# Rotary embedding on one core: sixteen positions to a partition, and four transfers that move two tiles each

## The chip, the core and the metric

The kernel runs on one core of a Trainium2 chip. The metric is the device time of one execution in microseconds. The engines named below are TensorE (PE, matmuls; its weight loads are PEld), VectorE (DVE), ScalarE (ACT), GpSimd (POOL) and SyncE (SP), which here only issues DMAs. The core has 16 DMA engines that move data between HBM and SBUF. SBUF is the working memory of 128 partitions; PSUM is the smaller memory that TensorE writes; GpSimd's work here is all in SBUF.

## The reference: what is computed

`x` is float32 of shape (16, 512, 1024): 16 batches, 512 positions, 16 heads of 64 values. `cos` and `sin` are (512, 32), one row for each position, the same for every batch and head. Each head's 64 values are two halves, x1 and x2:

```python
x1, x2 = (x[..., :half_dim].copy(), x[..., half_dim:].copy())
rotated = np.concatenate([x1 * cos - x2 * sin, x1 * sin + x2 * cos], axis=-1)
```

So the output is x times cos, plus x with its halves swapped times a signed sine (minus sine for the first half, plus sine for the second). 33.55 MB are read and 33.55 MB written, and every value needs two products and one sum.

## The kernel before

**Tiling.** There are 8 tiles of 4 MB, `x_tiles[0..7]`, each [128 partitions, 8 rows of 1024]. A partition holds 8 consecutive positions of one batch (64 partitions to a batch, two batches to a tile), so a partition's part of a tile is one run of 32 KB in HBM, and a whole tile is one contiguous block there. Five SBUF buffers hold the tiles; tiles 5, 6 and 7 reuse those of tiles 0, 1 and 2. Results are written over x in place and stored from there.

**Tables.** `tabs` holds 64 rows each of cos and sin (8 positions to a row). Two matmuls with the selection matrix `sel` (L115) spread them to all 128 partitions in PSUM. `tab` is one PSUM bank: half of it is the cosine table; behind that lies `snp`, the signed sine of the rows of group 2 alone. `sns` in SBUF is the signed sine of all rows, filled by ACT (L120, L121). PSUM is full: one bank for `tab`, six for `pp`, one for `ps`.

**The work on a tile.** `GROUPS` names stretches of rows (first row, number of rows) and `PLAN[t]` is an order written out by hand for each tile. An entry is a letter and a group:

- T (L148): POOL multiplies the swapped halves by `sns` into a T buffer. B (L148): the same on DVE, with `snp` from PSUM.
- P (L151): DVE multiplies x by the cosine into `pp` in PSUM. S (L153): DVE adds T and pp over x.
- A (L155): DVE multiplies x by the cosine in place. M (L160 to L163): for each chunk of 512 columns TensorE adds T and x into `ps` with two identity matmuls, and ACT copies the sum over x. There is one `ps`, so the chunks go one after the other: matmul of T, matmul of x, copy.

So a group is finished either by T (or B), P and S, or by T, A and M. The T buffers come from two pools of two, one for groups of two rows and one for groups of three: a T waits until the user of the buffer two before it is done. Each engine works its instructions in order.

**DMAs.** All x transfers are issued by SP in order, on one queue: the loads of tiles 0 (in four cuts) to 4, two tiny transfers `few` (L97), stores 0, 1, 2, loads 5, 6, 7, stores 3 to 6, and tile 7 in two cuts. A load into a reused buffer waits for the store that empties it. Every DMA takes the next of eight completion semaphores in turn and waits until the DMA that used it eight before has landed; the tiny transfers use up turns, so that a store does not inherit the semaphore of a transfer that is still far from done.

Of the kernel before, what the change touches and what calls it, by code (L numbers as in the profile page):

```python
# [11 lines left out]
@with_exitstack  # L12
def kernel(
    ctx: ExitStack,
    tc: tile.TileContext,
    x: bass.AP,
    cos: bass.AP,
    sin: bass.AP,
    num_heads: bass.AP,
    out: bass.AP,  # L20
):
    nc = tc.nc
    P = nc.NUM_PARTITIONS
    batch, seq, dim = x.shape
    nh = num_heads
    hd = dim // nh
    half = hd // 2


    BP = 2  # L30
    HP = P // BP
    R = seq // HP
    NT = batch // BP
    NB = 5
    C = 512
    GP = 3
    assert HP * R == seq and BP * NT == batch

    GROUPS = [(0, 3), (3, 3), (6, 2), (0, 2), (2, 2), (4, 2), (3, 2), (5, 3)]
    PLAN = ["T3 P3 T4 S3 P4 S4 B2 T5 P5 S5 P2 S2",
            "T0 T2 T1 P0 S0 P1 A2 M2 S1",
            "T0 T1 P0 B2 S0 P2 S2 P1 S1",
            "T2 T0 T1 A2 M2 P0 S0 P1 S1",
            "T0 T1 P0 B2 S0 A2 M2 P1 S1",
            "T0 T2 T1 P0 S0 A2 M2 P1 S1",
            "T2 T0 T1 A2 M2 P0 S0 P1 S1",
            "T0 T6 T7 P0 S0 P6 S6 P7 S7"]

    xv = x.rearrange("b (p r) d -> (b p) (r d)", r=R)
    xv = xv.rearrange("(t p) f -> t p f", p=P)
    ov = out.rearrange("b (p r) h d -> (b p) (r h d)", r=R)
    ov = ov.rearrange("(t p) f -> t p f", p=P)
    cosv = cos.rearrange("(p r) j -> p (r j)", r=R)
    sinv = sin.rearrange("(p r) j -> p (r j)", r=R)

    fixed = ctx.enter_context(tc.tile_pool(name="fixed", bufs=1))
    xin = ctx.enter_context(tc.tile_pool(name="xin", bufs=1))
    tpools = {n: ctx.enter_context(tc.tile_pool(name=f"tpool{n}", bufs=2)) for n in sorted({n for _, n in GROUPS})}  # L60
    ptab = ctx.enter_context(tc.tile_pool(name="ptab", bufs=1, space=bass.MemoryType.PSUM))
    pgrp = ctx.enter_context(tc.tile_pool(name="pgrp", bufs=1, space=bass.MemoryType.PSUM))
    prow = ctx.enter_context(tc.tile_pool(name="prow", bufs=1, space=bass.MemoryType.PSUM))

    ctx.enter_context(tc.manual_schedule())

    SYNC = mybir.DependencyInfo(mybir.DependencyClass.Sync, mybir.DependencyReason.DATA)

    def implied(inst, *others):
        for o in others:  # L70
            tc.declare_no_dep(inst.ins, o.ins, reason="implied by an earlier wait of the engine")

    bufs = [xin.tile([P, R * dim], FP32, name=f"x{i}_sb") for i in range(NB)]
    x_tiles = [bufs[t % NB] for t in range(NT)]
    loads = [[] for _ in range(NT)]
    stores = [[] for _ in range(NT)]

    def load(t, *cuts):
        for a, b in cuts or ((0, R),):
            loads[t].append(nc.sync.dma_start(out=x_tiles[t][:, a * dim:b * dim], in_=xv[t][:, a * dim:b * dim]))  # L80

    def store(t, *cuts):
        for a, b in cuts or ((0, R),):
            stores[t].append(nc.sync.dma_start(out=ov[t][:, a * dim:b * dim], in_=x_tiles[t][:, a * dim:b * dim]))

    load(0, (0, 1))
    tabs = fixed.tile([HP, 2, R * half], FP32, name="tabs")
    nc.scalar.dma_start(out=tabs[:, 1], in_=sinv)
    nc.scalar.dma_start(out=tabs[:, 0], in_=cosv)
    load(0, (1, 2), (2, 4), (4, 8))  # L90
    for t in range(1, NB):
        load(t)


    few = fixed.tile([1, 2], FP32, name="few")
    for i in range(2):
        nc.sync.dma_start(out=few[:, i:i + 1], in_=cosv[:1, i:i + 1])  # L97

    ident = fixed.tile([P, P], FP32, name="ident")
    nc.gpsimd.memset(ident, 0.0)  # L100
    nc.gpsimd.affine_select(  # L101
        out=ident, in_=ident, compare_op=ALU.not_equal, fill=1.0,
        base=0, pattern=[[-1, P]], channel_multiplier=1,
    )
    i64 = ident[:HP, :HP]
    sel = fixed.tile([HP, P], FP32, name="sel")
    nc.gpsimd.tensor_copy(out=sel.rearrange("k (b p) -> k b p", b=BP),  # L107
                          in_=bass.AP(tensor=i64.tensor, offset=i64.offset, ap=[i64.ap[0], [0, BP], [1, HP]]))

    tab = ptab.tile([P, C], FP32, name="tab")  # L110
    cos_ps = tab[:, :R * half].rearrange("p (r j) -> p r j", r=R)
    PR, PN = GROUPS[2]
    snp = tab[:, R * half:R * half + PN * hd].rearrange("p (r s j) -> p r s j", r=PN, s=2)
    sin_ps = pgrp.tile([P, GP * dim], FP32, name="pp")[:, :R * half].rearrange("p (r j) -> p r j", r=R)
    spread = [nc.tensor.matmul(out=o.rearrange("p r j -> p (r j)"), lhsT=sel, rhs=tabs[:, i],  # L115
                               start=True, stop=True) for i, o in ((1, sin_ps), (0, cos_ps))]
    sns = fixed.tile([P, R, 2, half], FP32, name="sns")
    signed = []
    for o, r0 in ((sns, 0), (snp, PR)):
        signed.append(nc.scalar.copy(out=o[:, :, 1, :], in_=sin_ps[:, r0:r0 + o.shape[1], :]))  # L120
        signed.append(nc.scalar.mul(out=o[:, :, 0, :], in_=sin_ps[:, r0:r0 + o.shape[1], :], mul=-1.0))  # L121

    def view(t, k):
        r0, n = GROUPS[k]
        return x_tiles[t][:, r0 * dim:(r0 + n) * dim]

    def cosb(k):
        r0, n = GROUPS[k]
        return bass.AP(tensor=cos_ps.tensor, offset=cos_ps.offset + r0 * half,
                       ap=[cos_ps.ap[0], [half, n], [0, 2 * nh], [1, half]])  # L130

    def snb(tab, r0, n):
        return bass.AP(tensor=tab.tensor, offset=tab.offset + r0 * hd, ap=[tab.ap[0], [hd, n], [0, nh], [1, hd]])

    def swapped(xr, n):
        return bass.AP(tensor=xr.tensor, offset=xr.offset + half, ap=[xr.ap[0], [hd, n * nh], [-half, 2], [1, half]])

    Ts, pps = {}, {}

    def emit(t, op):  # L140
        o, k = op[0], int(op[1])
        r0, n = GROUPS[k]
        xr = view(t, k)
        if o in "TB":
            m = GP if t == 0 and o == "T" else n
            Ts[t, k] = tpools[m].tile([P, m * dim], FP32, name="T")[:, :n * dim]
            eng, tb = (nc.gpsimd, snb(sns, r0, n)) if o == "T" else (nc.vector, snb(snp, r0 - PR, n))
            return [eng.tensor_tensor(out=Ts[t, k], in0=swapped(xr, n), in1=tb, op=ALU.mult)]  # L148
        if o == "P":
            pps[t, k] = pgrp.tile([P, GP * dim], FP32, name="pp")[:, :n * dim]  # L150
            return [nc.vector.tensor_tensor(out=pps[t, k], in0=xr, in1=cosb(k), op=ALU.mult)]  # L151
        if o == "S":
            return [nc.vector.tensor_tensor(out=xr, in0=Ts[t, k], in1=pps[t, k], op=ALU.add)]  # L153
        if o == "A":
            return [nc.vector.tensor_tensor(out=xr, in0=xr, in1=cosb(k), op=ALU.mult)]  # L155
        made = []
        for c in range(n * dim // C):
            ps = prow.tile([P, C], FP32, name="ps")
            xc = xr[:, c * C:(c + 1) * C]
            made.append(nc.tensor.matmul(out=ps, lhsT=ident, rhs=Ts[t, k][:, c * C:(c + 1) * C],  # L160
                                         start=True, stop=False))
            made.append(nc.tensor.matmul(out=ps, lhsT=ident, rhs=xc, start=False, stop=True))  # L162
            made.append(nc.scalar.copy(out=xc, in_=ps))  # L163
        return made

    done = [[] for _ in range(NT)]

    def compute(t):
        met = False
        for op in PLAN[t].split():  # L170

            met = met or op[0] in "SA"
            for i in emit(t, op):
                if t > 0 and met and op[0] != "T":
                    implied(i, *loads[t])
                if t >= NB:
                    implied(i, *loads[t - NB], *stores[t - NB], *done[t - NB])
                done[t].append(i)

    for t in range(NB):  # L180
        compute(t)
        if t < NT - NB:
            store(t)
    for t in range(NB, NT):
        load(t)
    for t in range(NT - NB, NB):
        store(t)
    for t in range(NB, NT):
        compute(t)
        store(t, *((0, 5), (5, 8)) if t == NT - 1 else ())  # L190


# [33 lines left out]
```

## Time and profile before

| what | value |
|---|---|
| median of 3 runs | 162.48 us (162.45 to 162.59) |
| the profiled execution's own time | 162.54 us |
| its span | 160.8 us |
| DVE busy | 138.4 us (86%) |
| POOL busy | 130.2 us (81%) |
| PE busy | 58.4 us (36%) |
| ACT busy | 14.1 us (9%) |
| moved, mean rate over the span | 67.25 MB, 418 GB/s |
| mean granted TensorE clock | 0.795 |

Busy time is that of instructions; the span runs from the first to the last of them. In the slices the span is cut into 40 equal parts of 4.02 us, and a digit is the busy share in tenths. The lines for groups of instructions give busy time and the mean duration in ns, then the engine's idle time before them and what ended it. A DMA is issued by its queue (SPq) and its bytes follow later, behind everything issued earlier; it has landed when its semaphore is complete.

### The profile page before, as it was taken

The numbers are of one execution on the slowest core, as the hardware profiler recorded it, in microseconds if no ns is written. First come the engines' busy times: TensorE is split into PE (matmuls) and PEld (weight loads), VectorE is DVE, ScalarE is ACT, GpSimd is POOL, SyncE is SP. The second block draws the span as 40 slices with busy tenths as digits, with TensorE's granted clock in tenths as the row PEclk, the third lists the DMA queues.
The fourth block names the chain that finished last, engine by engine and source line by source line (L and its number), as shares of the span: only waits on it lengthen the run. The fifth ranks groups of instructions, "written<-read, shape, count | busy, mean of one in ns | idle before, by whom it ended". The sixth has DMA issues, their size and how long they took to land.

```text
span 160.8 us, 390 instructions
## 1 busy us (share of the span) xinstructions
PE 58.4 (36%) x84; PEld 18.3 (11%) x84; DVE 138.4 (86%) x48; ACT 14.1 (9%) x25; POOL 130.2 (81%) x29
## 2 busy tenths in 40 slices
PE   0500000022388803088701368896868630000000
PEld 0200000010122100022201022222222200000000
DVE  0069999999999999999999999999999999999200
ACT  3110000000011110011200011002121210000000
POOL 2299929999999899995999299999999999991000
PEclk9999999999999995557995555559999995555555
DMA  5999999999999999999999999999999999999994
GB/s 159 383 444 481 391 448 465 391 432 473 400 400 506 400 391 481 432 391 481 432 391 448 465 391 432 473 400 408 497 400 400 483 416 408 473 424 400 428 417 199
DMA packets 3046, 67.25 MB, mean 418 GB/s; under 512 B 357, under 2 KB 485, under 8 KB 741
## 3 DMA queue, kind: packets, MB, share of 16 engines
q1 hardware_dynamic: 2884, 67.11, 97.8%
q10 hardware_dynamic: 160, 0.13, 0.3%
q14 instruction: 2, 0.01, 0.0%
HBM read 33.69 MB, written 33.55 MB: 418 GB/s over the span
## 4 chain that ended last, share of the span: by engine, by line
DVE 81%; issue 5%; POOL 3%; DMA 3%; PE 1%; ACT 0%; DVEq 0%
DVE x_sb L153 38%; DVE pp L151 36%; DVE x_sb L155 6%; POOL T L148 3%; DMA tabs<-in_sin_dram 3%; DVE T L148 1%; PE pp L115 1%; ACT sns L120 0%; ACT sns L121 0%; DVEq L153 0%; DVEq L151 0%
## 5 line engine op out<-in xcount | busy, mean ns | idle before, releaser
L148 POOL TENSOR_TENSOR T<-x_sb,sns 128x3072 f32<-128x3072 f32 (+1 forms) x22 | 129.2, 5910 | 14.3 <-DMA x_sb<-in_x_dram 6.2
L151 DVE TENSOR_TENSOR pp<-x_sb,tab 128x3072 f32<-128x3072 f32 (+1 forms) x20 | 60.8, 3040 | 9.0 <-ACT tab L121 8.5
L153 DVE TENSOR_TENSOR x_sb<-T,pp 128x3072 f32<-128x3072 f32 (+1 forms) x20 | 60.7, 3033 | 2.4 <-POOL T L148 0.8
L160 PE MATMUL ps<-T,ident 128*128 128x512 f32 x40 | 30.4, 849 | 50.1 <-POOL T L148 30.8
L162 PE MATMUL ps<-x_sb,ident 128*128 128x512 f32 x40 | 28.7, 809 | 15.8 <-DVE x_sb L155 15.8
L163 ACT COPY x_sb<-ps 128x512 f32<-128x512 f32 x20 | 11.7, 585 | 110.3 <-PE ps L162 110.3
L160 PEld LDWEIGHTS ps<-T,ident 128*128 128x128 f32 x40 | 7.6, 238 | 72.9 <-POOL T L148 32.3
L162 PEld LDWEIGHTS ps<-x_sb,ident 128*128 128x128 f32 x40 | 9.7, 252 | 31.6 <-DVE x_sb L155 20.1
L155 DVE TENSOR_TENSOR x_sb<-x_sb,tab 128x2048 f32<-128x2048 f32 x5 | 11.4, 2281 | 0.0
L148 DVE TENSOR_TENSOR T<-x_sb,tab 128x2048 f32<-128x2048 f32 x3 | 6.8, 2281 | 0.0
L115 PE MATMUL pp<-tabs,sel 64*128 64x256 f32 x2 | 1.2, 696 | 5.2 <-DMA tabs<-in_sin_dram 5.2
L120 ACT ACT_TABLE_LOAD x1 | 1.3, 1283 | 1.9 <-issue 1.9
L115 PE MATMUL tab<-tabs,sel 64*128 64x256 f32 x2 | 1.2, 710 | 0.4 <-DMA tabs<-in_cos_dram 0.4
L115 PEld LDWEIGHTS pp<-tabs,sel 64*128 64x128 f32 x2 | 0.5, 307 | 5.2 <-issue 5.2
L120 ACT COPY sns<-pp 128x256 f32<-128x256 f32 x1 | 0.4, 372 | 3.2 <-PE pp L115 3.2
L115 PEld LDWEIGHTS tab<-tabs,sel 64*128 64x128 f32 x2 | 0.5, 306 | 1.2 <-DMA tabs<-in_cos_dram 1.2
L100 POOL MEMSET ident<- 128x128 f32 x1 | 0.2, 204 | 0.3 <-POOLq L207 0.3
L121 ACT ACTIVATE sns<-pp 128x256 f32<-128x256 f32 x1 | 0.4, 390 | 0.0
L101 POOL TENSOR_SCALAR_AFFINE_SELECT ident<-ident 128x128 f32<-128x128 f32 x1 | 0.3, 292 | 0.1
L107 POOL COPY sel<-ident 64x128 f32<-64x128 f32 x1 | 0.3, 283 | 0.1
L207 POOL MEMSET const-float32-0.0<- 128x1 f32 x1 | 0.1, 98 | 0.2 <-issue 0.2
L120 ACT COPY tab<-pp 128x64 f32<-128x64 f32 x1 | 0.2, 197 | 1.0 <-PE tab L115 1.0
(4 smaller groups left out, 0.5 us busy)
## 6 DMA issues: line engine op xcount, KB each, us to landing
x_sb<-in_x_dram SPq DMA_DIRECT2D x7, 4096.0 KB, 29.1
out_dram<-x_sb SPq DMA_DIRECT2D x7, 4096.0 KB, 18.9
out_dram<-x_sb SPq DMA_DIRECT2D x1, 2560.0 KB, 13.4
x_sb<-in_x_dram SPq DMA_DIRECT2D x1, 2048.0 KB, 11.8
out_dram<-x_sb SPq DMA_DIRECT2D x1, 1536.0 KB, 10.1
x_sb<-in_x_dram SPq DMA_DIRECT2D x2, 512.0 KB, 3.9
x_sb<-in_x_dram SPq DMA_DIRECT2D x1, 1024.0 KB, 7.4
tabs<-in_sin_dram ACTq DMA_DIRECT2D x1, 64.0 KB, 4.3
```

Source lines behind the costliest of these rows:

```text
L101: nc.gpsimd.affine_select(out=ident, in_=ident, compare_op=ALU.not_equal, fill=1.0, base=0, pattern=[[-1, P]], channel_multiplier=1,)
L107: nc.gpsimd.tensor_copy(out=sel.rearrange("k (b p) -> k b p", b=BP), in_=bass.AP(tensor=i64.tensor, offset=i64.offset, ap=[i64.ap[0], [0, ...
L115: spread = [nc.tensor.matmul(out=o.rearrange("p r j -> p (r j)"), lhsT=sel, rhs=tabs[:, i], start=True, stop=True) for i, o in ((1, sin_ps ...
L120: signed.append(nc.scalar.copy(out=o[:, :, 1, :], in_=sin_ps[:, r0:r0 + o.shape[1], :]))
L121: signed.append(nc.scalar.mul(out=o[:, :, 0, :], in_=sin_ps[:, r0:r0 + o.shape[1], :], mul=-1.0))
L148: return [eng.tensor_tensor(out=Ts[t, k], in0=swapped(xr, n), in1=tb, op=ALU.mult)]
L151: return [nc.vector.tensor_tensor(out=pps[t, k], in0=xr, in1=cosb(k), op=ALU.mult)]
L153: return [nc.vector.tensor_tensor(out=xr, in0=Ts[t, k], in1=pps[t, k], op=ALU.add)]
L155: return [nc.vector.tensor_tensor(out=xr, in0=xr, in1=cosb(k), op=ALU.mult)]
L160: made.append(nc.tensor.matmul(out=ps, lhsT=ident, rhs=Ts[t, k][:, c * C:(c + 1) * C], start=True, stop=False))
L162: made.append(nc.tensor.matmul(out=ps, lhsT=ident, rhs=xc, start=False, stop=True))
L163: made.append(nc.scalar.copy(out=xc, in_=ps))
```

## The change

A partition now holds 16 positions of one batch, 32 partitions to a batch, four batches to a group of 128 partitions. A group is two tiles: tile t is half `t % 2` of group `t // 2`. A partition's part of a group is one run of 64 KB in HBM, and that of one tile is a run of 32 KB, 64 KB from the next.

- The five buffers become one tile of five slots. Tiles 0 to 3 lie in slots 1 to 4, tile 4 in slot 0, and later tiles 5, 6 and 7 in slots 1, 2 and 3, so that the two tiles of a group are always neighbours.
- Load 2+3, store 0+1, load 6+7 and store 4+5 are one transfer each. Store 0+1 is issued after tile 1's work and store 4+5 after tile 5's; tiles 2 and 3 are usable when both have landed, and so are tiles 6 and 7.
- The tables are loaded as 32 rows of 16 positions each, sine in partitions 0 to 31 and cosine in 32 to 63. Two sine matmuls of 256 columns go to the `ps` bank, one cosine matmul of 512 columns fills the `tab` bank. `snp` is gone: B reads `sns` in SBUF, as T does. The copies into `sns` come in two pairs, one for each half.
- `sel` is made by a memset and two selects in place of a copy from `ident`.
- `PLAN[1]` and `PLAN[5]` become "T2 T0 T1 A2 M2 P0 S0 P1 S1".
- There are six tiny transfers in place of two.

```diff
-    BP = 2
+    BP = 4
     HP = P // BP
-    R = seq // HP
-    NT = batch // BP
+    R = seq // HP // 2
+    NT = 2 * batch // BP
...
-            "T0 T2 T1 P0 S0 P1 A2 M2 S1",
+            "T2 T0 T1 A2 M2 P0 S0 P1 S1",
...
-            "T0 T2 T1 P0 S0 A2 M2 P1 S1",
+            "T2 T0 T1 A2 M2 P0 S0 P1 S1",
...
-    bufs = [xin.tile([P, R * dim], FP32, name=f"x{i}_sb") for i in range(NB)]
-    x_tiles = [bufs[t % NB] for t in range(NT)]
+    F = R * dim
+    slots = xin.tile([P, NB * F], FP32, name="x_sb")
+    first = [(t + 1) % NB * F if t < NB else (t - NB + 1) * F for t in range(NT)]
+    x_tiles = [slots[:, f:f + F] for f in first]
...
+    def sides(v, t, a, b):
+        h = t % 2 * F
+        return slots[:, first[t] + a * dim:first[t] + b * dim], v[t // 2][:, h + a * dim:h + b * dim]
...
-    tabs = fixed.tile([HP, 2, R * half], FP32, name="tabs")
-    nc.scalar.dma_start(out=tabs[:, 1], in_=sinv)
-    nc.scalar.dma_start(out=tabs[:, 0], in_=cosv)
+    tabs = fixed.tile([2 * HP, 2 * R * half], FP32, name="tabs")
+    nc.scalar.dma_start(out=tabs[:HP], in_=sinv)
+    nc.scalar.dma_start(out=tabs[HP:], in_=cosv)
     load(0, (1, 2), (2, 4), (4, 8))
-    for t in range(1, NB):
-        load(t)
+    load(1)
+    load(2, (0, 2 * R))
+    load(4)
...
-    few = fixed.tile([1, 2], FP32, name="few")
-    for i in range(2):
+    NF = 6
+    few = fixed.tile([1, NF], FP32, name="few")
+    for i in range(NF):
...
+    sel = fixed.tile([2 * HP, BP, HP], FP32, name="sel")
+    nc.gpsimd.memset(sel, 0.0)
+    for h in range(2):
+        nc.gpsimd.affine_select(
+            out=sel, in_=sel, compare_op=ALU.not_equal, fill=1.0,
+            base=-h * HP, pattern=[[0, BP], [-1, HP]], channel_multiplier=1,
+        )
...
-    snp = tab[:, R * half:R * half + PN * hd].rearrange("p (r s j) -> p r s j", r=PN, s=2)
...
+    cos_ps = ptab.tile([P, C], FP32, name="tab")
+    sin_ps = prow.tile([P, C], FP32, name="ps").rearrange("p (r j) -> p r j", j=half)
+    sns = fixed.tile([P, 2 * R, 2, half], FP32, name="sns")
...
+    spread(sin_ps[:, :R], 0, 0, R * half)
+    spread(cos_ps, 1, 0, C)
+    spread(sin_ps[:, R:], 0, R * half, C)
+    for h in range(2):
+        rows = slice(h * R, (h + 1) * R)
+        nc.scalar.copy(out=sns[:, rows, 1, :], in_=sin_ps[:, rows, :])
+        nc.scalar.mul(out=sns[:, rows, 0, :], in_=sin_ps[:, rows, :], mul=-1.0)
...
-            eng, tb = (nc.gpsimd, snb(sns, r0, n)) if o == "T" else (nc.vector, snb(snp, r0 - PR, n))
-            return [eng.tensor_tensor(out=Ts[t, k], in0=swapped(xr, n), in1=tb, op=ALU.mult)]
+            eng = nc.gpsimd if o == "T" else nc.vector
+            return [eng.tensor_tensor(out=Ts[t, k], in0=swapped(xr, n), in1=snb(t, k), op=ALU.mult)]
...
     for t in range(NB):
         compute(t)
-        if t < NT - NB:
-            store(t)
-    for t in range(NB, NT):
-        load(t)
-    for t in range(NT - NB, NB):
-        store(t)
-    for t in range(NB, NT):
-        compute(t)
-        store(t, *((0, 5), (5, 8)) if t == NT - 1 else ())
+        if t == 1:
+            store(0, (0, 2 * R))
+        if t == 2:
+            store(2)
+    load(5)
+    load(6, (0, 2 * R))
+    store(3)
+    compute(5)
+    store(4, (0, 2 * R))
+    compute(6)
+    store(6)
+    compute(7)
+    store(7, (0, 5), (5, 8))
```

## The prediction

> **What bounds the kernel now.** I read the page's slices first, then the groups of instructions by shape, then who waits for whom, then the order of time around the late tiles. The page's slices, queue and chain:
>
> ```profile
> span 160.8 us, 390 instructions
> ...
> DVE  0069999999999999999999999999999999999200
> ...
> POOL 2299929999999899995999299999999999991000
> ...
> DMA  5999999999999999999999999999999999999994
> ...
> q1 hardware_dynamic: 2884, 67.11, 97.8%
> ...
> DVE 81%; issue 5%; POOL 3%; DMA 3%; PE 1%; ACT 0%; DVEq 0%
> ```
>
> The DMA engines are full from the second slice to the last but one: 67.11 MB in one unbroken stream set the end. The chain runs through DVE, but DVE ends at 149.75 and the queue works on for 10 us, so DVE has slack, as long as each store is issued before the queue runs dry. The reader should look for when it would.
>
> ```profile
> L148 POOL TENSOR_TENSOR T<-x_sb,sns 128x3072 f32<-128x3072 f32 x14 | 93.6, 6703 | 8.2 <-DMA x_sb<-in_x_dram 6.2 <-DVE x_sb L153 2.0
> L151 DVE TENSOR_TENSOR pp<-x_sb,tab 128x3072 f32<-128x3072 f32 x14 | 47.0, 3360 | 0.3
> L148 POOL TENSOR_TENSOR T<-x_sb,sns 128x2048 f32<-128x2048 f32 x8 | 36.1, 4521 | 6.1 <-ACT sns L121 5.5 <-PE ps L160 0.6
> L155 DVE TENSOR_TENSOR x_sb<-x_sb,tab 128x2048 f32<-128x2048 f32 x5 | 11.4, 2281 | 0.0
> L148 DVE TENSOR_TENSOR T<-x_sb,tab 128x2048 f32<-128x2048 f32 x3 | 6.8, 2281 | 0.0
> ```
>
> All DVE products take one operand from SBUF and one (tab or pp) from PSUM; POOL's take both from SBUF. Who holds the stores up:
>
> ```profile
> SPq L84 <- DVE x_sb L153: 91.8, 8, 16.7
> SPq L84 <- ACT x_sb L163: 24.7, 3, 11.0
> ```
>
> Three stores wait for ACT, that is for the TensorE path (M) of a tile. The last copies of tile 4 and those of tile 5, in order of time (start, duration):
>
> ```profile
> 104.09 0.58 ACT L163 COPY x_sb<-ps 128x512 f32<-128x512 f32 x1 [3.87 <-PE ps L162]
> 108.55 0.58 ACT L163 COPY x_sb<-ps 128x512 f32<-128x512 f32 x1 [3.87 <-PE ps L162]
> 111.27 0.58 ACT L163 COPY x_sb<-ps 128x512 f32<-128x512 f32 x1 [2.14 <-PE ps L162]
> 113.93 0.58 ACT L163 COPY x_sb<-ps 128x512 f32<-128x512 f32 x1 [2.07 <-PE ps L162]
> 116.59 0.58 ACT L163 COPY x_sb<-ps 128x512 f32<-128x512 f32 x1 [2.07 <-PE ps L162]
> 119.25 0.58 ACT L163 COPY x_sb<-ps 128x512 f32<-128x512 f32 x1 [2.07 <-PE ps L162]
> ```
>
> A chunk takes 4.45 us at granted clock 0.5 (84.6 to 108.5) and 2.66 us at 1.0 (108.5 to 132.4). Tile 5 is complete at 119.83.
>
> **The change, part by part.** The sum is made against the profiled execution: 162.54 us, a span of 160.8 and 1.7 around it; it lies 0.06 above the median 162.48.
>
> *Longer runs.* In the trace's packet records a stretch of eight 32 KB packets per engine takes 9.68 us between the ends of two stores, 1209 ns each; at the slope between the 20 KB and 32 KB stores a packet has 4 to 9 ns of its own. Four double transfers save 32 packets per engine, 0.13 to 0.29 us, and four completion packets of 9 ns. If a 64 KB run still goes as two packets, only the latter goes. I take 0.2 us saved.
>
> *Start.* The two table loads halve their rows (46 ns each at 1 KB): nothing to 0.1 us. The cosine matmul grows from 256 to 512 columns, from 1.22 us to at most the 2.07 us of the M pairs, so DVE's first product starts near 8.95 instead of 8.53; it ends at 11.25, still before POOL's first T at 11.65, which hides it by 0.4 us. Uncovered it would cost those 0.4 us of DVE. The third small matmul and the second pair of sns copies end by 11 us; tile 1's first T, at 23.8, is the first to need them. POOL loses a copy (0.28) and gains a memset and two selects (0.2, 0.29 each), all before the sine table lands at 5.05. Four more tiny DMAs hold SP until tile 1 lands at 23.66; the store behind them is due at 47. On one engine they take at most 0.15 us.
>
> *Joined loads.* Tile 2 becomes usable at 43.1 instead of 33.4, POOL wants it at 41.7: 1.4 us late, absorbed where POOL waits for its buffers until 75.2. Tile 6 comes at 111 instead of 101.4, POOL wants it at 109.7, so the last DVE product ends 0.9 us later; the last store has 4 us of queue ahead of it. Load 5 now waits for the double store (72), load 6+7 for store 2 (82), each with 9 us of queue left.
>
> *Joined stores.* Store 0+1 waits for tile 1, 46 to 48.5 by the new order, which puts A2 first; the queue runs to 51.9. The tight one is store 4+5: store 3 leaves the queue at about 120, and a transfer's first packet comes 1.0 us after its issue (0.74 to 1.75 at the start), so tile 5 must be complete by 119. Its A2 comes earlier, but M of tile 5 queues behind M of tile 4, so its end is 119.83 less 1.79 us for each chunk run at the full clock instead of the half one. This trace has three such episodes: tile 1 ran three chunks slow, tile 3 two, tile 4 four. With two or three (116.3, 118.0) there is no gap, with four a gap of 0.8. The Trainium skill, "TensorE: Matmul & The Clock Gate", Part 1, has the full clock come after one busy window of about 3.4 us, a window that runs freely against the kernel. By that alone at most two chunks would be slow and there would be no gap; the trace's tiles 1 and 4 disagree with three and four, so I count in chunks.
>
> So far: 162.54 - 0.2, or 162.3.
>
> *B reads its table from SBUF.* The three B products on DVE (tiles 0, 2, 4) now take both operands from SBUF, while POOL streams from the same tiles. No row shows DVE so. Lower end: 2281 ns as now, cost nothing; a gain has no row to come from, as A and P of that shape take the same. Middle: POOL's pace for both operands in SBUF, 4521 ns, 2.2 us more each. Upper end: one engine waits until the other's whole instruction is over. The nearest row by its operands is POOL's, twice as slow at the same size, and POOL is busy 81% of the span, so I lean upward and take the upper end. The Trainium skill, "SBUF — State Buffer", section "Who interferes with whom", says that a DVE instruction with two SBUF inputs and a GpSimd instruction that reads SBUF exclude each other for the whole instruction; no row here shows it either way, and by it the sum would be this upper end.
>
> The waits, walked with the row durations: tile 0's B is ready at 18.7 and POOL's third T ends at 20.6: 1.9 us. Tile 2's B is ready at 51.3; POOL, with the late tile 2, runs T1 from 49.8 to 56.5: 5.2 us. The rest of tile 2 took 14.85 us (51.34 to 66.19) and ends at 73.6, its store's first packet at 74.6; the double store ran out at 71.7: a gap of 2.9. POOL's T1 of tile 4 waits for tile 3's last sum, 89.4, and runs to 96.1; B is ready at 92.8: 3.3 us more, the lag is 10.8. A2 of tile 4 ends at 103.8 instead of 93.0, DVE's tile 5 at 126.3, and M of tile 5 26.75 us after M of tile 4 starts with four slow chunks (93.08 to 119.83): 130.6, with three 128.8, with two 127.0. I take the middle episode, three: first packet at 129.8, while store 3 ran out at 123.0 (120.1 plus the first gap): a gap of 6.8. After that nothing starves: DVE ends near 160.5, the queue reaches the last store at 165.
>
> Sum: 162.54 - 0.2 + 2.9 + 6.8 = 172.0; 170.3 with two slow chunks, 173.8 with four.
>
> **Rivals.** *No contention on B, runs a little cheaper:* 162.3. For it: DVE's duration is the same wherever it reads now. It ends inside 0.2%, which is about what a measurement of this kernel can tell from no change; with the full 0.33 us it is just faster. It decides if B stays at 2.3 us and tile 5 is complete before 119. *No contention, store 4+5 late:* four slow chunks, 163.1; five, 164.9. *B at POOL's pace:* tile 2 ends at 70.6, in time; M of tile 5 6.6 us later, 124.6 with three slow chunks: a gap of 5.5, 167.8 (166 to 169.6). *POOL's next T goes ahead of the waiting B* in tiles 2 and 4: up to 4.5 us more each, 176 to 181. *The longer runs do nothing:* 0.2 more on any of these.
>
> **How the numbers follow.** Whole waits 0.60, POOL's pace 0.13, POOL ahead 0.05, no contention with a late store 0.07, without 0.15. I predict 172.0. The likeliest case's own range is 169.5 to 174.5. Down to 163.0 the range takes in the slower paces and the late store; left out are the 0.15 of no gap and the 0.05 above. Slower 0.85; of the 0.15 I give 0.10 to the same and 0.05 to faster.
>
> **What would show it.** Right: B's three instructions on DVE much over 2.3 us, or idle before them that ends with POOL; dips in the DMA slices near 73 and 124 to 130 us; the store of tile 2 issued near 73.6 and store 4+5 near 129. Wrong: B at 2.28 us and DMA at 9 in all slices; then the time is 162.3, and the slow chunks alone decide the rest. Half as many packets on q1 for the double transfers, at twice the duration less a few ns, would confirm the run length.

## The result, and the profile after

The changed kernel takes 170.51 us (median of four executions, 170.30 to 174.13), the kernel before 162.53 beside it. The ratio is 1.0481, with a 95% interval of 1.0453 to 1.0508: 4.8% slower. The forecast was 172.0. The profiled execution takes 170.30 us with a span of 168.5, 7.7 us more than before. (The one at 174.13 ran at a lower granted clock, 0.757, and is left out of the ratio, as is one at 170.45 of the experiment with short products below, at 0.750.)

From the page of the changed kernel, the slices and the main queue:

```profile
span 168.5 us, 393 instructions
...
DVE  0047999999999999999999999999999989999910
...
POOL 3089969999799999559499999989999999992000
PEclk9999999999999555555799555599999996555555
DMA  5999999996998995958999899988949979889994
...
q1 hardware_dynamic: 2316, 67.11, 94.3%
```

A slice is now 4.21 us. The DMA row was full and now has dips, the deepest at slice 17 (72 to 76 us, counted from 0) and slice 29 (122 to 126). A packet counts in the slice in which it starts, and those of the joined transfers last 2.4 us, so that a low slice with the next one over the mean rate (slice 15: 249 GB/s, then 498) is no dip. The reader should look at what a late DVE does: the queue runs dry. In stretches of time (start and end, the busy time of each engine and the granted clock; the DMA share and the GB/s are the last two columns):

```profile
54.00:72.00 18.00, 2.07 (x2) 0.50 (x2) 17.79 (x6) 0.00 (x0) 15.70 (x3) 0.53 0.94 408
72.00:75.00 3.00, 0.00 (x0) 0.00 (x0) 3.00 (x2) 0.00 (x0) 1.49 (x1) 0.50 0.42 175
75.00:124.00 49.00, 27.43 (x43) 8.61 (x43) 48.38 (x16) 6.44 (x11) 45.40 (x8) 0.75 1.00 417
124.00:128.00 4.00, 3.05 (x6) 0.95 (x6) 4.00 (x2) 0.58 (x1) 4.00 (x1) 1.00 0.62 262
```

The two dry stretches are those of store 2 and of store 4+5. What changed on the engines, by groups of one shape:

```profile
L174 POOL TENSOR_TENSOR T<-x_sb,sns 128x3072 f32<-128x3072 f32 x14 | 93.6, 6697 | 8.6 <-DVE x_sb L179 7.5 <-DMA x_sb<-in_x_dram 1.0
L174 POOL TENSOR_TENSOR T<-x_sb,sns 128x2048 f32<-128x2048 f32 x8 | 40.7, 5101 | 8.2 <-ACT sns L145 6.7 <-DMA x_sb<-in_x_dram 1.5
L174 DVE TENSOR_TENSOR T<-x_sb,sns 128x2048 f32<-128x2048 f32 x3 | 15.5, 5173 | 0.0
L181 DVE TENSOR_TENSOR x_sb<-x_sb,tab 128x2048 f32<-128x2048 f32 x5 | 11.4, 2278 | 0.0
```

B on DVE went from 2281 to 5173 ns, and POOL's products of two rows from 4521 to 5101. All other products are unchanged to a few ns. How this comes about is to be read in tile 2, in order of time (start, duration):

```profile
49.85 6.67 POOL L174 TENSOR_TENSOR T<-x_sb,sns 128x3072 f32<-128x3072 f32 x1
...
52.85 5.81 DVE L174 TENSOR_TENSOR T<-x_sb,sns 128x2048 f32<-128x2048 f32 x1
...
56.47 6.58 POOL L174 TENSOR_TENSOR T<-x_sb,sns 128x2048 f32<-128x2048 f32 x1
```

POOL's product ends at 56.52. B, issued at 52.85, ends at 58.67, 2.15 after that, about the length that it has alone. POOL's next product, 4.52 us long when undisturbed, is issued at 56.47 and takes 6.58: it stands 2.1 us behind B. The trace has the same in the other two: B ends at 24.52 where POOL ends at 22.37, and at 98.11 where POOL ends at 95.96, 2.15 us each time. The three waits are inside the durations (B's idle time before it is 0.0); they are what is over 2.28: 1.85, 3.53 and 3.30 us.

Where the 7.7 us went, by the packets' ends and starts at each border of the stream (the completion packets of one transfer against the first packets of the next, the latest engine): 0.8 us before store 0+1 (issued at 52.1, the queue out at 52.3), 1.9 before store 2 (issued at 73.5, out at 72.5), 2.4 before store 4+5 (issued at 126.6, out at 125.2). The fourth part was not foreseen: at 82.9 and at 111.4 us, close to the two turns of the queue, from stores to loads and back, all 16 engines have packets up to 1.5 us too long, 30 us in sum, 1.9 us for each engine. Together 7.0 us; the rest lies in small differences at both ends and is not assigned.

### The profile page after: what moved, and what is told of

Its sections match the earlier page's. It is cut to its first block, busy times and chain, and to the rows that moved or that the text cites. A ratio compares the mean times of both kernels' runs of the same rounds, so it can differ in the third digit from the quotient of the medians.

```text
span 168.5 us, 393 instructions
## 1 busy us (share of the span) xinstructions
PE 58.4 (35%) x86; PEld 17.9 (11%) x86; DVE 147.0 (87%) x48; ACT 14.2 (8%) x25; POOL 135.4 (80%) x31
## 4 chain that ended last, share of the span: by engine, by line
DVE 78%; issue 9%; DMA 3%; POOL 3%; PE 1%; ACT 0%; ACTq 0%; DVEq 0%
DVE x_sb L179 35%; DVE pp L177 35%; DVE x_sb L181 7%; DMA tabs<-in_cos_dram 3%; POOL T L174 3%; DVE T L174 3%; PE tab L136 1%; PE ps L136 0%; ACTq L103 0%; ACT sns L144 0%; DVEq L179 0%; ACT sns L145 0%
## 5 line engine op out<-in xcount | busy, mean ns | idle before, releaser
L174 POOL TENSOR_TENSOR T<-x_sb,sns 128x3072 f32<-128x3072 f32 (+1 forms) x22 | 133.9, 6116 | 16.8 <-DVE x_sb L179 7.5
L188 PE MATMUL ps<-x_sb,ident 128*128 128x512 f32 x40 | 27.9, 788 | 19.3 <-DVE x_sb L181 19.3
L174 DVE TENSOR_TENSOR T<-x_sb,sns 128x2048 f32<-128x2048 f32 x3 | 15.5, 5173 | 0.0
L136 PE MATMUL ps<-tabs,sel 32*128 32x256 f32 x4 | 2.4, 702 | 4.4 <-DMA tabs<-in_sin_dram 4.4
L136 PE MATMUL tab<-tabs,sel 32*128 32x512 f32 x2 | 2.1, 1136 | 0.5 <-DMA tabs<-in_cos_dram 0.5
L136 PEld LDWEIGHTS ps<-tabs,sel 32*128 32x128 f32 x4 | 1.0, 306 | 4.4 <-issue 4.4
L144 ACT COPY sns<-ps 128x256 f32<-128x256 f32 x2 | 0.8, 376 | 5.3 <-PE tab L136 5.3
L145 ACT ACTIVATE sns<-ps 128x256 f32<-128x256 f32 x2 | 0.8, 404 | 0.0
L120 POOL TENSOR_SCALAR_AFFINE_SELECT sel<-sel 64x128 f32<-64x128 f32 x2 | 0.6, 302 | 0.1
L136 PEld LDWEIGHTS tab<-tabs,sel 32*128 32x128 f32 x2 | 0.5, 308 | 1.2 <-DMA tabs<-in_cos_dram 1.2
## 6 DMA issues: line engine op xcount, KB each, us to landing
x_sb<-in_x_dram SPq DMA_DIRECT2D x3, 4096.0 KB, 48.5
```

What stands on the lines that cost most here:

```text
L120: nc.gpsimd.affine_select(out=sel, in_=sel, compare_op=ALU.not_equal, fill=1.0, base=-h * HP, pattern=[[0, BP], [-1, HP]], channel_multipl ...
L136: nc.tensor.matmul(out=o, lhsT=sel[h * HP:(h + 1) * HP].rearrange("k b p -> k (b p)"), rhs=tabs[h * HP:(h + 1) * HP, a:b], start=True, sto ...
L144: nc.scalar.copy(out=sns[:, rows, 1, :], in_=sin_ps[:, rows, :])
L145: nc.scalar.mul(out=sns[:, rows, 0, :], in_=sin_ps[:, rows, :], mul=-1.0)
```

## The experiments

Two causes were to be told apart: that B and POOL exclude each other, and that the joined stores come late by themselves, helped by a start that the profile showed to be late. All times are medians, with the ratio to the kernel before on the same chip.

**B from PSUM.**

```diff
-            return [eng.tensor_tensor(out=Ts[t, k], in0=swapped(xr, n), in1=snb(t, k), op=ALU.mult)]
+            return [eng.tensor_tensor(out=Ts[t, k], in0=swapped(xr, n), in1=(snb if o == "T" else psb)(t, k), op=ALU.mult)]
```

(`psb` is the same pattern of reads over the cosine bank.)

> The changed kernel with one edit: the three B products on DVE take their second operand from the cosine bank in PSUM instead of sns in SBUF. So the B rows are multiplied by the wrong table; shapes, steps and counts are the same. Theory (DVE with two SBUF operands and POOL exclude each other): B falls from 5.17 us to 2.28 us, store 2 is issued near 68 and the queue does not run dry there. The time is 162.3 to 162.6 where three or fewer chunks of tiles 4 and 5 run at the half clock, 165 with four. Rival (the joined stores alone, or the start that is 1.8 us late, make the kernel slow): B may fall, but the time stays at 168 or more.

Measured: 165.56 us, 1.0159 (1.0101 to 1.0217); its executions are 163.68, 165.48, 165.64 and 165.85. Its B, and the copies of tile 4 and the first of tile 5:

```profile
L179 DVE TENSOR_TENSOR T<-x_sb,tab 128x2048 f32<-128x2048 f32 x3 | 6.8, 2280 | 0.0
```

```profile
97.12 0.58 ACT L194 COPY x_sb<-ps 128x512 f32<-128x512 f32 x1 [14.55 <-PE ps L193]
101.57 0.58 ACT L194 COPY x_sb<-ps 128x512 f32<-128x512 f32 x1 [3.87 <-PE ps L193]
106.03 0.58 ACT L194 COPY x_sb<-ps 128x512 f32<-128x512 f32 x1 [3.87 <-PE ps L193]
110.48 0.58 ACT L194 COPY x_sb<-ps 128x512 f32<-128x512 f32 x1 [3.87 <-PE ps L193]
113.20 0.58 ACT L194 COPY x_sb<-ps 128x512 f32<-128x512 f32 x1 [2.14 <-PE ps L193]
```

B is back at 2280 ns and store 2 is issued at 68.1, while the queue still works. But the four chunks of tile 4 are slow here (4.45 us apart), and store 4+5 is issued only at 121.79, with the queue out at 119.4 to 120.4. So the exclusion of the two engines is one part, about 5 us of the 8; the joined store is another, and here it makes the kernel slower by itself. The execution at 163.68 is about 2 us shorter than the others, close to the 1.8 us of one slow chunk; it has no trace.

**The kernel before, with B from SBUF.**

```diff
-            eng, tb = (nc.gpsimd, snb(sns, r0, n)) if o == "T" else (nc.vector, snb(snp, r0 - PR, n))
+            eng, tb = (nc.gpsimd, snb(sns, r0, n)) if o == "T" else (nc.vector, snb(sns, r0, n))
```

> The kernel before with one edit: B reads its signed sine from sns in SBUF instead of snp in PSUM; layout, loads, stores and tables stay. Theory: B takes 4 to 6 us, DVE ends near 159 instead of 149.75, store 2 leaves a gap of about 1.3 us and the last three stores gaps of 0.8 to 1.9 us: about 167.2. Rival (the layout or the joined transfers): B stays near 2.3 us or its wait is hidden, and the time is 162.5.

Measured: 166.24 us, 1.0244 (1.0203 to 1.0285), 1 us under the expected value. DVE ends at 158.6, as expected, but the loss is made up otherwise: the gaps by the latest engine are 0.5 us before store 2 and 0.1 and 0.6 before the two cuts of store 7, and 1.8 us for each engine are long packets at the two turns, which the expectation did not have.

```profile
L148 DVE TENSOR_TENSOR T<-x_sb,sns 128x2048 f32<-128x2048 f32 x3 | 16.0, 5319 | 0.0
```

One operand moved from PSUM to SBUF, nothing else, costs the old kernel 3.6 us. The layout and the joined transfers have no part in this. One rival is left: in every run with a long B, its operand in SBUF is `sns`, the table that POOL reads too. A table of its own in SBUF was not tried, so these runs don't tell two operands in SBUF from one table read by both.

**Stores one by one.**

```diff
-        if t == 1:
-            store(0, (0, 2 * R))
-        if t == 2:
-            store(2)
+        if t < 3:
+            store(t)
...
+    store(4)
     compute(5)
-    store(4, (0, 2 * R))
+    store(5)
```

> The changed kernel with stores 0+1 and 4+5 issued one by one, each as its tile is done; the loads stay joined and B stays in SBUF. Theory: the gap before store 4+5 (2.4 us) and the one before store 0+1 (0.8 us) go, the gap at store 2 stays at 2 to 3 us, and DVE, still 10.7 us late, now holds up the stores of tiles 6 and 7: 167.5 to 168.5, and no spread from the chunks. Rival (the joined stores are the whole loss): 162.5 to 163.

Measured: 168.60 us, 1.0374 (1.0356 to 1.0392), 0.1 us over the upper edge of the expected range, with four executions within 0.4 us. The gap before store 2 is 2.4 us, those before the two cuts of store 7 are 0.5 us each, and the long packets at the two turns are still there. The joined stores cost the changed kernel 1.9 us; the larger part stays.

**Both edits.**

> Both edits: B reads the cosine bank in PSUM (the B rows use the wrong table) and stores 0+1 and 4+5 are issued one by one. Theory: no wait of the two engines on each other and no store that comes late: 162.3 to 162.5 in every execution, whatever the chunks do; what is left of the change is the layout, the joined loads and the late start. Rival (rows 64 KB apart in HBM are slower, or the late start shows): more than 163.

Measured: 162.41 us, 0.9994 (0.9982 to 1.0006), the same as before. Of its ten executions nine lie at 162.24 to 162.62 and one at 163.07, so the time is not the expected one in every execution. The DMA row is full but for four slices, and these lie in the joined loads (28 to 44 us and 92 to 112), whose long packets count where they start:

```profile
DMA  5999999699699999999999997996999999999994
```

So the new layout, with rows 64 KB apart in the single transfers, the joined loads, their longer runs and the later start together make no difference that this measurement can tell when the stores are in time; the run does not separate a small cost of one from a small gain of another.

| | stores joined | stores one by one |
|---|---|---|
| B from SBUF | 170.51 | 168.60 |
| B from PSUM | 165.56 | 162.41 |
| B from PSUM, early start | 162.36 | |

Against 162.41, B from SBUF alone costs 6.2 us and the joined stores alone 3.2; together they cost 8.1, less than the sum.

**An early start.** In the changed kernel the first T is late: the first copy into `sns` waits until all three matmuls are done.

```profile
8.19 0.37 ACT L144 COPY sns<-ps 128x256 f32<-128x256 f32 x1 [5.26 <-PE tab L136]
...
8.93 4.50 POOL L174 TENSOR_TENSOR T<-x_sb,sns 128x2048 f32<-128x2048 f32 x1 [6.74 <-ACT sns L145]
```

Before, POOL's first T started at 7.15:

```profile
7.15 4.50 POOL L148 TENSOR_TENSOR T<-x_sb,sns 128x2048 f32<-128x2048 f32 x1 [5.50 <-ACT sns L121]
```

The edit, on top of B from PSUM with the stores joined, puts the two sine matmuls into two tiles:

```diff
-    sin_ps = prow.tile([P, C], FP32, name="ps").rearrange("p (r j) -> p r j", j=half)
+    sin_ps = [pool.tile([P, w], FP32, name=name)[:, :R * half].rearrange("p (r j) -> p r j", j=half)
+              for pool, w, name in ((pgrp, GP * dim, "pp"), (prow, C, "ps"))]
...
```

> The kernel of the B-from-PSUM experiment (B rows use the cosine bank, so the wrong table), with the two sine matmuls in different PSUM tiles, so that the first copies into sns wait for the first matmul alone. Theory (the late first T, 8.93 instead of 7.15, is what pushes tile 5 over the edge in that experiment, 121.8 instead of 119.8): the first T starts before 7.2, tile 5 is complete at 118 to 120, and the time falls from 165.6 to 162.3 with three slow chunks, 163.1 with four. Rival (the joined store 4+5 is late whatever the start): 165 or more.

Measured: 162.36 us, 0.9998 (0.9978 to 1.0018). The first T starts at 7.07:

```profile
5.91 0.37 ACT L145 COPY sns<-pp 128x256 f32<-128x256 f32 x1 [2.99 <-PE pp L137]
...
7.07 4.50 POOL L180 TENSOR_TENSOR T<-x_sb,sns 128x2048 f32<-128x2048 f32 x1 [4.89 <-DMA x_sb<-in_x_dram]
```

Eight of its ten executions lie at 162.24 to 162.41, two at 163.39 and 163.49. In the profiled one two chunks of tile 4 are slow and store 4+5 is issued at 116.2. The pair at 163.4 fits the late store that the forecast put at 163.1 with four slow chunks; no trace was taken of these two. So the median falls by 3.2 us through one store, but not by the start alone: tile 4's first copy comes 1.9 us earlier than in B from PSUM (95.20 instead of 97.12), and the other 3.6 us by which store 4+5 is earlier are two slow chunks fewer. Whether the start sets the number of slow chunks is not shown.

**Short products on POOL.**

```diff
+            if o == "T" and (t, k) in ((0, 5), (2, 1), (4, 1)):
+                tb = snb(t, k)
+                return [eng.tensor_tensor(
+                    out=Ts[t, k][:, r * dim:(r + 1) * dim], in0=swapped(xr[:, r * dim:(r + 1) * dim], 1),
+                    in1=bass.AP(tensor=tb.tensor, offset=tb.offset + r * hd, ap=[tb.ap[0], [hd, 1], [0, nh], [1, hd]]),
+                    op=ALU.mult) for r in range(n)]
```

(T5 of tile 0 has two rows, T1 of tiles 2 and 4 three.)

> The changed kernel with one edit: the three POOL products that B finds running (T5 of tile 0, T1 of tiles 2 and 4) are issued row by row, one instruction of about 2.2 us for each row; the work is the same. Theory (the engine that comes second waits until the other's instruction is over, and the waiting one is next): B waits for one short piece, at most 2.2 us, and its mean falls from 5.17 us to between 2.3 and 4.5 us; the kernel gets 2 to 5 us faster than 170.5, 165.5 to 168.5. Rival (the two engines share the bandwidth of one port): POOL streams on all the same, B stays near 5.2 us and the time near 170.5. Rival (POOL's next instruction goes ahead of the waiting B): B grows over 5.2 us.

Measured: 166.93 us, 1.0260 (1.0226 to 1.0295), 3.6 us faster than the changed kernel. B by its group, and POOL's second and third row of tile 2's T1:

```profile
L180 DVE TENSOR_TENSOR T<-x_sb,sns 128x2048 f32<-128x2048 f32 x3 | 11.5, 3846 | 0.0
```

```profile
52.12 2.34 POOL L176 TENSOR_TENSOR T<-x_sb,sns 128x1024 f32<-128x1024 f32 x1
```

```profile
54.42 4.41 POOL L176 TENSOR_TENSOR T<-x_sb,sns 128x1024 f32<-128x1024 f32 x1
```

B is issued at 52.92, between the two. It waits for the second row (54.47) and ends at 56.61, 2.14 later; the third row, issued at 54.42, takes 4.41 us instead of 2.3. With sharing, POOL's rows would have gone on and B would have kept its 5.2 us. The waiting instruction is next, and what it waits for is one instruction. The three B take 4.27, 3.69 and 3.57 us, so the first gains nothing: it finds a row just begun. Store 2 is now issued just in time and its gap is gone.

**One B alone in SBUF.** As B from PSUM, but tile 4's B reads `sns`.

> The changed kernel with B in SBUF for tile 4 alone; the B rows of tiles 0 and 2 read the cosine bank in PSUM (the wrong table). Theory: only tile 4's B is long, about 5.6 us; store 2 is in time and the queue has one dry stretch, before store 4+5, whose M starts 5.2 us later than before: complete near 123.3 with three slow chunks, 125 with four, so 166 to 168. The slow DMA packets near 83 and 111 us (1.9 us in the changed kernel's trace) should be gone if they come with the dry stretch at store 2. Rival (the loss comes from the first two B): the time is that of the experiment with all B in PSUM, 165.6.

Measured: 165.30 us, 1.0188 (1.0142 to 1.0233).

```profile
L179 DVE TENSOR_TENSOR T<-x_sb,sns 128x2048 f32<-128x2048 f32 x1 | 5.6, 5576 | 0.0
L179 DVE TENSOR_TENSOR T<-x_sb,tab 128x2048 f32<-128x2048 f32 x2 | 4.6, 2280 | 0.0
```

Only that one is long. The time is 0.7 under the lower expectation, since just two chunks were slow in the profiled execution (the second copy 4.45 us after the first, the third 2.66), and store 4+5 was issued at 121.4; of the four executions three lie at 165.15 to 165.39, and one at 166.97 is longer by about one slow chunk, without a trace. By its time alone this run can't be told from B from PSUM with four slow chunks; the rows tell. The slow packets near 83 us are gone and those near 108 are small (1.4 us summed over the engines).

**A version that computes the reference.** The layout and the joined loads, the early start, the stores one by one, and the signed sine for B in the last quarter of the `ps` bank, with M in chunks of 384 columns:

```diff
+    CM = 384
...
+    row = prow.tile([P, C], FP32, name="row")
+    snp = row[:, CM:CM + PN * hd].rearrange("p (r s j) -> p r s j", r=PN, s=2)
...
-        for c in range(n * dim // C):
-            ps = prow.tile([P, C], FP32, name="ps")
+        for c in range(0, n * dim, CM):
+            w = min(CM, n * dim - c)
+            ps = row[:, :w]
...
```

> A version of the changed kernel that keeps the layout and the joined loads and computes the reference: M works in chunks of 384 columns, so that the last quarter of the ps bank holds the signed sine for B; the two sine matmuls go to different tiles; stores 0+1 and 4+5 are issued one by one. Theory: no wait between DVE and POOL, early start, no store late: 162.0 to 162.4, the same as before or up to 0.3% faster, the longer runs of the joined loads being worth about 0.1 us. Rival (longer M, about 12 instead of 10.6 us a tile at full clock, holds up a store): more than 163.

Measured: 163.42 us, 1.0051 (1.0033 to 1.0069): a miss. No store came late. In the profiled execution fifteen engines finish at 159.34, as in the both-edits run, where all are done by 159.36; one finishes at 160.13. It had two slow packets, 0.39 us at 121.0 and 0.45 us at 127.4. The second starts right behind an 8 KB packet of the instruction queue (127.08); what the first one met is not recorded. The program has 489 instructions instead of 395. So no version here beats the kernel before.

## Why the prediction was right, and where it was not

*Whole waits on B.* Right: the likeliest case came, with waits of 1.9, 3.5 and 3.3 us against 1.9, 5.2 and 3.3. The Trainium skill, "SBUF — State Buffer", section "Who interferes with whom", gave the rule that the second to start waits for the first's whole instruction; the ends 2.15 us apart and the run with short products agree. The middle wait was shorter because B was ready 1.6 us later, at 52.85; POOL's end came as predicted, 56.5, so DVE left tile 2 at 73.4 (forecast 73.6).

*Start.* Wrong. The prediction had DVE's first product hidden and looked at the second pair of copies, not the first. The step that failed is the reading of who releases the first copy: it waited until 8.19, behind the cosine and the second sine matmul, and the first T came at 8.93 instead of 7.15. In the changed kernel it has a part in the 0.8 us before store 0+1: tile 1 ended at 52.08, where the prediction said 46 to 48.5. 1.8 us of that are the start and another 1.8 the wait of tile 0's B, which the prediction had but did not carry into this store (with B from PSUM tile 1's first copy comes at 36.35 instead of 38.13), and all four chunks were slow. By these sizes the gap needs all three; with the stores one by one, the same start and the same wait, two slow chunks let tile 1 end at 48.5.

*Gap at store 2.* 1.9 instead of 2.9: the issue time was right, but the queue ran out later, behind the gap that was missed.

*Gap at store 4+5.* 2.4 instead of 6.8, the largest miss of a size. The forecast took three slow chunks; there were about two (105.73, 109.98, then 2.66 apart), and tile 5 was ready at 126.57, against 127.0 foreseen for two: 2.2 us earlier than with three. And the queue ran out at 125.2 instead of 123.0, another 2.2, held back mostly by the slow packets.

*Slow packets at the turns.* Not in the prediction: 1.9 us.

*Longer runs.* The 64 KB run goes as one packet: the trace has 512 packets of 65,536 bytes, the shortest 2418 ns against 2426 for two of 32 KB, and q1 has 568 packets fewer. Load 2+3 takes 19.35 us from end to end instead of 19.44. The 0.2 us taken for it lies inside the interval of the run with both edits, from 0.3 us less to 0.1 more than the kernel before, so that run neither shows nor excludes it.

*The clock.* The Trainium skill, "TensorE: Matmul & The Clock Gate", Part 1, has one busy window of about 3.4 us bring the full clock. The two slow chunks in tile 4 of the changed kernel can fit that; the four in its tile 1, and the four in tile 4 of B from PSUM, don't. A slow chunk is 4.45 us with a pause of 0.68 us in it, and the number of slow ones differs between tiles and between the traced kernels; what sets it stays open. Counting chunks was the right unit.

The errors have opposite signs: the two gaps were taken 5.4 us too large, and 2.7 us at the start and at the turns were missed. So the 172.0 came nearer to the measured time than its terms did, which is luck; the mechanism, B's wait and the two late stores behind it, is not.

## What to carry to other kernels

Where two engines work side by side, ask of each edit what memory each operand comes from: in these runs a DVE product with both operands in SBUF and a POOL product, with its operands in SBUF too, wait for each other's whole instruction, and one operand of the DVE product in PSUM avoids it; where that can't be, short instructions on POOL limit the wait. A transfer joined from two tiles becomes due with its later half, so count the slack of the queue at that point, in the worst pace of the engine that finishes the tile. And when an edit moves a table, look at who releases its first reader.

## What the runs showed of the hardware that was not expected

- In four kernels (the changed kernel, the old kernel with B from SBUF, stores one by one, short products) the turns from stores to loads and from loads to stores, near 82 and 111 us, cost all 16 engines long packets: 13 to 14 and 15 to 19 us summed over them. In the others (before, B from PSUM, both edits, early start, one B, the version that computes the reference) the same turns cost at most 2.4. In each of the four, the queue had run dry before: in three just before store 2, some 10 us ahead of the first turn, in short products only before store 0+1, some 30 us ahead. A dry queue starts all engines together: in these four their first packets of store 2 lie within 0.15 us of each other, in the others they are spread over 0.4 us or more. Whether being in step is the cause stays open; it was not tried.
- In each trace an 8 KB packet of the instruction queue falls between 126 and 145 us, and 0.3 us later one engine has a packet 0.35 to 0.45 us too long, which it carries to the end: in the kernel before, the last engine finishes at 159.55 and the others by 159.09.
